# Gate products of a decoder step: one dense pair, seven pairs as seven-product units, projections ahead of them

## The chip, the cores and the metric

The kernel runs on one core of one Trainium2 chip. Its engines are TensorE (PE: matmuls and transposes into PSUM), VectorE (DVE), ScalarE (ACT), GpSimd (POOL) and SyncE (SP); SP and POOL also issue the DMA transfers. Each engine works through its own list of instructions in order and waits on semaphores. The metric is the device time of one execution in microseconds; the number of a kernel is the median of several executions.

## The reference

One inference step of a decoder layer on 1024 prompt positions and 8 sample tokens (1032 columns), model width 1024, all in fp32:

```python
xn = rmsnorm(x)
z = xn @ w_in                          # q, k, v | u, v_a | g_a | g_b
a_out = u * (tril(W_s) v_a + b)        # in chunks of 128 positions, 512 wide
b_out = dilated window attention       # 256 wide; sample tokens read caches
merged = sigmoid(ga) * (a_out @ w_proj_a) + sigmoid(gb) * (b_out @ w_proj_b)
h = x + merged @ w_out
up = rmsnorm(h) @ w_up                 # then a causal convolution of width 3
h = h + (gelu(gate) * val) @ w_down
y = rmsnorm(h)
```

The change is in the line `merged`: ga and gb are 1024 x 1032 each, made from 8 blocks of 128 output rows.

## The kernel before

Activations lie transposed: 128 features on the partitions, 1032 positions on the free axis; width 1024 is 8 such rows (KT = 8). An fp32 product is made of three matmuls (high x high, high x low, low x high), so each weight tile `wraw` is split by ACT into `whi` (a cast, L187) and by DVE into `wlo` (a subtraction, L188), and each operand likewise (`xnh`/`xnl`, `ah`/`al` for branch A, `bh`/`bl` for branch B, `mh` for the merged rows). `unit` (L208 to 210) runs one block of columns over all k; `dense` runs the blocks of a whole row: 384, 384 and 264 columns (`TB`), or 512, 260 and 260 (`TP`).

The up projection uses another form, `pair_unit` (L275 to 278). Two blocks of output rows are made together as a 2 x 2 block product in seven products in place of eight, in the order of `ORDER`: the weights enter as four parts and four sums (`ws`, L251; s1 to s4), the operand as blocks 11, 12, 21, 22 and the differences t1 to t4 (`tx`, L325), all split into `xc` tiles (cast L333 on ACT, subtraction L334 on DVE) by `combos`, after `scale_rows` (L307) has multiplied the rows by the norm. Columns come in two halves p (`HALF`) of 2 x 256 and 2 x 260 columns. Each of the seven products is 2 halves x 4 k x 3 matmuls of 256 or 260 columns; one unit is 168 matmuls.

The gate stage runs per block j: `gate` for g_a, then the projection of `a_out` with w_proj_a (4 k) whose eviction multiplies by the gate; after all eight, branch B's rows are split (`bh`, `bl`; the 8 sample columns come from `osam` by a transpose `bst`, copied to `bs`), and the eight g_b gates follow with w_proj_b (2 k) between them. Their evictions multiply, add and split the merged rows into `mh`. Then the output product, `h_pass(0)` and `h_pass(1)`.

Other work is cut into steps in the queue `side`; `tick` takes steps from it at the rate `pace` while the products are written out, and `drain` takes all that are left. In the gate stage these steps are the attention of the sample tokens: `load_keys` (tiles `ck`, `cq` from the caches), `key_scores` (L833, L834), `sample_softmax` (`sp`, L841 to L845), `sample_turn` (`pp`, `pT`), `load_values`, `sample_product` (`pv`, an ACT copy `os` and four small POOL stores to `osam`) and `sample_out` (`bst`). A scheduler then sets the order on each engine from the program's order and its data. `touch` (L92) is a copy of one element on DVE: it makes a DMA into a reused tile wait for the tile's last reader. PSUM is two rings of four banks, `pmm` for products and `pxx` for the rest; wraw has 3 buffers, whi and wlo 6 each.

## Time and profile before

| | us |
|---|---|
| median of 3 executions | 1525.52 (1525.44 to 1526.32) |
| profiled execution, whole | 1525.51 |
| its span, first to last instruction | 1523.8 |
| PE busy | 1500.1 (98%) |
| DVE busy | 901.1 (59%) |
| ACT busy | 590.2 (39%) |
| POOL busy | 114.3 (7%) |

In the chain of work that ended last PE holds 94%, DMA 3%, DVE 2%. The start-to-start distance of matmuls is the cost of a matmul; the duration in a row is longer, since matmuls overlap.

### The profile page before, as it was taken

Reading aid. Unit: us, or ns where it says so; the run is one execution under the profiler, and the core shown is the slowest. Engines: PE = TensorE matmul, PEld = TensorE weight load, DVE = VectorE, ACT = ScalarE, POOL = GpSimd, SP = SyncE. Lnnn points to the kernel's source line nnn. Section 1 sums busy time; section 2 is a strip of 40 time slices with the busy share of each in tenths; the row PEclk is TensorE's granted clock in tenths of the full one; section 3 lists DMA queues with packets and bytes.
Section 4 is the critical chain, followed back from the end, with each engine's and each line's share of the span. In section 5 each row is a group of like instructions: output and inputs, shape, how many; then the busy total and the mean of one; then the engine's idle time right before and its main releaser. Section 6 shows DMA issues by size and latency. Waiting matters only on the chain.

```text
span 1523.8 us, 25982 instructions
## 1 busy us (share of the span) xinstructions
PE 1500.1 (98%) x10518; PEld 1435.9 (94%) x10518; DVE 901.1 (59%) x1768; ACT 590.2 (39%) x1223; POOL 114.3 (7%) x275
## 2 busy tenths in 40 slices
PE   7999999999999999999999999999999999999997
PEld 7988999899999799998899999999999999899997
DVE  5444435435757224545687887878788856534436
ACT  6444333344121212333456655444445542212114
POOL 1100123132000200002000300000000001000000
PEclk9999999999999999999999999999999999999999
DMA  8300122133116311126443322222222246423302
GB/s 253 117 19 29 54 73 79 46 83 107 36 39 187 101 40 49 39 59 204 143 140 105 91 67 74 84 83 72 83 84 84 77 127 216 119 75 90 117 22 112
DMA packets 169420, 140.11 MB, mean 92 GB/s; under 512 B 7394, under 2 KB 154053, under 8 KB 169293
## 3 DMA queue, kind: packets, MB, share of 16 engines
q1 hardware_dynamic: 160277, 115.41, 25.0%
q0 software_dynamic: 8992, 23.04, 5.0%
q8 instruction: 82, 1.34, 0.4%
q14 instruction: 37, 0.30, 0.1%
q10 hardware_dynamic: 32, 0.01, 0.0%
HBM read 107.97 MB, written 30.68 MB: 91 GB/s over the span
## 4 chain that ended last, share of the span: by engine, by line
PE 94%; DMA 3%; DVE 2%; ACT 1%; issue 1%; SPq 0%; ACTq 0%; DVEq 0%
PE mm L208 19%; PE mm L209 19%; PE mm L210 19%; PE mm L277 8%; PE mm L275 8%; PE mm L278 8%; PE s L561 2%; PE po L586 2%; PE pt L576 1%; DMA gt<-g_d 1%; DMA x<-in_x_prompt_dram 1%; PE mm L711 1%; PE pv L871 1%; PE mm L713 1%; PE mm L712 1%; PE mm L1420 1%
## 5 line engine op out<-in xcount | busy, mean ns | idle before, releaser
L187 ACT CAST whi<-wraw 128x512 fp32r<-128x512 f32 (+2 forms) x275 | 158.4, 586 | 390.8 <-PE mm L209 281.1
L208 PE MATMUL mm<-xnh,whi 128*128 128x384 f32 (+3 forms) x936 | 308.6, 330 | 0.0
L277 PE MATMUL mm<-xc,whi 128*128 128x256 f32 (+1 forms) x1064 | 300.4, 282 | 0.0
L278 PE MATMUL mm<-xc,wlo 128*128 128x256 f32 (+1 forms) x1064 | 300.3, 282 | 0.0
L275 PE MATMUL mm<-xc,whi 128*128 128x256 f32 (+1 forms) x1064 | 300.2, 282 | 0.0
L210 PE MATMUL mm<-xnh,wlo 128*128 128x384 f32 (+3 forms) x936 | 299.6, 320 | 0.0
L209 PE MATMUL mm<-xnl,whi 128*128 128x384 f32 (+3 forms) x936 | 299.6, 320 | 0.0
L188 DVE TENSOR_TENSOR wlo<-wraw,whi 128x512 fp32r<-128x512 f32 (+2 forms) x275 | 174.2, 643 | 71.4 <-ACT whi L187 67.6
L277 PEld LDWEIGHTS mm<-xc,whi 128*128 128x128 f32 x1064 | 201.2, 189 | 0.0
L275 PEld LDWEIGHTS mm<-xc,whi 128*128 128x128 f32 x1064 | 201.1, 189 | 0.0
L278 PEld LDWEIGHTS mm<-xc,wlo 128*128 128x128 f32 x1064 | 200.8, 189 | 0.0
L208 PEld LDWEIGHTS mm<-xnh,whi 128*128 128x128 f32 x936 | 176.1, 188 | 12.3 <-issue 6.8
L209 PEld LDWEIGHTS mm<-xnl,whi 128*128 128x128 f32 x936 | 176.2, 188 | 3.7 <-issue 0.7
L210 PEld LDWEIGHTS mm<-xnh,wlo 128*128 128x128 f32 x936 | 175.9, 188 | 3.6 <-issue 0.7
L208 PE MATMUL mm<-gh,whi 128*128 128x384 f32 (+1 forms) x456 | 146.2, 322 | 4.7 <-ACT gh L1340 4.7
L209 PE MATMUL mm<-gl,whi 128*128 128x384 f32 (+1 forms) x456 | 147.3, 323 | 0.9 <-DVE gl L1341 0.8
L210 PE MATMUL mm<-gh,wlo 128*128 128x384 f32 (+1 forms) x456 | 146.4, 321 | 0.0
L1372 DVE TENSOR_TENSOR hD<-mm,hD 128x384 f32<-128x384 f32 (+1 forms) x96 | 48.0, 509 | 84.5 <-PE mm L210 84.3
L1312 DVE SCALAR_TENSOR_TENSOR cv<-up,cw,cv 128x1024 f32<-128x1024 f32 x76 | 97.1, 1278 | 0.8 <-issue 0.8
L208 PEld LDWEIGHTS mm<-gh,whi 128*128 128x128 f32 x456 | 86.4, 190 | 5.5 <-ACT gh L1340 5.5
L187 ACT CAST whi<-ws 128x512 fp32r<-128x512 f32 x76 | 47.2, 621 | 108.6 <-PE mm L277 107.4
L209 PEld LDWEIGHTS mm<-gl,whi 128*128 128x128 f32 x456 | 86.7, 190 | 1.7 <-DVE gl L1341 1.1
(295 smaller groups left out, 2599.0 us busy)
## 6 DMA issues: line engine op xcount, KB each, us to landing
wraw<-in_w_up_dram SPq DMA_DIRECT2D x50, 512.0 KB
wraw<-in_w_in_dram SPq DMA_DIRECT2D x42, 512.0 KB
gt<-g_d SPq DMA_DIRECT2D x22, 516.0 KB
g_d<-cv SPq DMA_DIRECT2D x19, 516.0 KB
wraw<-in_w_out_dram SPq DMA_DIRECT2D x16, 512.0 KB
wraw<-in_w_down_dram SPq DMA_DIRECT2D x24, 320.0 KB
xT_d<-xT POOLq DMA_DIRECT2D x8, 516.0 KB, 5.3
hD<-hT_d POOLq DMA_DIRECT2D x8, 516.0 KB, 7.4
```

Source lines behind the costliest of these rows:

```text
L187: nc.scalar.copy(hi[:, :n, :], src)
L188: nc.vector.tensor_tensor(lo[:, :n, :], src, hi[:, :n, :].bitcast(F32), op=ALU.subtract)
L208: nc.tensor.matmul(ps[:, :n], hi[k], xh, start=(k == 0), stop=False)
L209: nc.tensor.matmul(ps[:, :n], hi[k], xl, start=False, stop=False)
L210: nc.tensor.matmul(ps[:, :n], lo[k], xh, start=False, stop=(k == nk - 1))
L275: nc.tensor.matmul(ps, hi[:, k, :], xh, start=(first and k == 0), stop=False, skip_group_check=not first)
L277: nc.tensor.matmul(ps, hi[:, k, :], xl, start=False, stop=False, skip_group_check=not first)
L278: nc.tensor.matmul(ps, lo[:, k, :], xh, start=False, stop=(k == 3), skip_group_check=not first)
L561: nc.tensor.matmul(ps[:, off:off + ncol], qf[hr, qc:qc + P], kf[hr, kc:kc + ncol], start=True, stop=True)
L586: nc.tensor.matmul(po[:, gi * 64:gi * 64 + 64], pt[:, j * P:(j + 1) * P], vt[:, n, 64 * h:64 * h + 64], start=(bi == 0), stop=(bi == nb - 1))
L1312: nc.vector.scalar_tensor_tensor(c[:, :m], up[:, i:i + m], wi, c[:, :m], op0=ALU.mult, op1=ALU.add)
L1372: nc.vector.tensor_tensor(hT[j][:, cs], ps[:, :n], hT[j][:, cs], op=ALU.add)
```

## The change

The gates of block 0 stay as they were (both dense now with `TB`). For the blocks 1 to 7 the pair (g_a, g_b) of one block is one seven-product unit on the normalised x. Its operand `xn` is made in the same way as that of the up projection: rows of x are read back from memory (`xT_d` into `xr`, on SP), scaled by norm and `rb`, and turned into 28 `xc` tiles and the differences `tx`, as steps of `side` during the projections.

All eight products with w_proj_a, then all eight with w_proj_b, now come ahead of these units (`project`). The projected rows of blocks 1 to 7 are copied out of PSUM by ACT (`pr`) and stored to memory (`pa_d`, `pb_d`), and read back (`pl`) in the unit of their block, where two sigmoids, two multiplications and an addition over 1032 columns merge them. The merged rows are stored to `m_d`, read back by halves and split into `mh` while unit 7 and the first output pass run. The convolution parameters and histories move from the projections to the units; the rows of branch B become steps (`b_rows`). The function `pair_unit` is the same as for the up projection.

```diff
-            if (name, p, q) not in tsum:
+            if (id(X), name, p, q) not in tsum:
...
-    ma = []
-    ma.append(gate(3328))
-    for j in range(KT):
-        if j + 1 < KT:
-            ma.append(gate(3328 + (j + 1) * P))
-        if j == 0:
-            while len(a_hi) < 4:
-                side.popleft()()
-            pace[1] = 1.0
-            side.append(conv_params)
-            side.append(lambda: (load_hist(0), load_hist(1)))
-            side.append(lambda: None)
-            for i in range(6):
-                side.append(lambda i=i: turn_hist(i))
-            side.append(sample_out)
-        w = load_w(w_proj_a[0], 0, 4, j * P)
-        def post(b, t0, n, ps, sg=ma[j]):
-            nc.vector.tensor_tensor(sg[:, t0:t0 + n], ps[:, :n], sg[:, t0:t0 + n], op=ALU.mult)
-        dense(w, a_hi, a_lo, post)
...
+    sg0 = [gate(3328), gate(4352)]
+    while len(a_hi) < 4:
+        side.popleft()()
+    xR = [{}, {}]
+    xn = {}
+    def load_rows(R, p, i, src, after, ks=(0, 1)):
+        t0, n = HALF[p]
+        R[p][i] = ftile("xr")
+        touch(R[p][i], after)
+        for k in ks:
+            nc.sync.dma_start(R[p][i][:, 2 * k * n:(2 * k + 2) * n], src[2 * i + k][:, t0:t0 + 2 * n])
+    def x_loads(p, q):
+        for i in (q, q + 2):
+            load_rows(xR, p, i, xT_d, a_hi[3].bitcast(F32))
+    def x_steps(p, q):
+        yield lambda: x_loads(p, q)
+        yield idle
+        yield lambda: scale_rows(xR, p, q, (0, 1), lambda kt: nrm[:, kt:kt + 1], rb)
+        for names in (("11", "t1"), ("t2", "21"), ("t3", "22"), ("t4",)):
+            yield lambda names=names: combos(xn, xR, p, q, names)
...
-    mt = []
-    for j in range(KT):
-        sg = gate(4352 + j * P, False)
-        w = load_w(w_proj_b[0], 0, 2, j * P)
-        mj = [ftile("mh", F32R) for _ in range(2)]
-        def post(b, t0, n, ps, sg=sg, mj=mj, ma_j=ma[j]):
-            cs = slice(t0, t0 + n)
-            nc.vector.tensor_tensor(sg[:, cs], ps[:, :n], sg[:, cs], op=ALU.mult)
-            nc.vector.tensor_tensor(sg[:, cs], sg[:, cs], ma_j[:, cs], op=ALU.add)
-            mh, ml = m_parts(mj, t0, n)
-            nc.scalar.copy(mh, sg[:, cs])
-            nc.vector.tensor_tensor(ml, sg[:, cs], mh.bitcast(F32), op=ALU.subtract)
-        dense(w, b_hi, b_lo, post, blocks=TP)
-        mt.append(mj)
+    first_steps = list(side) + [sample_out, lambda: b_rows(0), lambda: b_rows(1)]
+    side.clear()
+    second_steps = [s for p in range(2) for q in range(2) for s in x_steps(p, q)]
+    late = max(0, len(first_steps) - 14)
+    side.extend(first_steps[:late])
+    for i in range(max(len(first_steps) - late, len(second_steps))):
+        side.extend(first_steps[late + i:late + i + 1])
+        side.extend(second_steps[i:i + 1])
+    pace_for(48)
+    m_d, pa_d, pb_d = (dpool.tile([KT, P, T], F32, tag=name, name=name) for name in ("m_d", "pa_d", "pb_d"))
+    def project(w2d, nk, ahi, alo, dst, first):
+        for j in range(KT):
+            w = load_w(w2d, 0, nk, j * P)
+            pr_ = first if j == 0 else ftile("pr")
+            def post(b, t0, n, ps, j=j, pr_=pr_):
+                cs = slice(t0, t0 + n)
+                if j == 0:
+                    nc.vector.tensor_tensor(pr_[:, cs], ps[:, :n], pr_[:, cs], op=ALU.mult)
+                else:
+                    nc.scalar.copy(pr_[:, cs], ps[:, :n])
+            dense(w, ahi, alo, post)
+            if j > 0:
+                nc.sync.dma_start(dst[j], pr_[:, :T])
+    project(w_proj_a[0], 4, a_hi, a_lo, pa_d, sg0[0])
+    while len(b_hi) < 2:
+        side.popleft()()
+    project(w_proj_b[0], 2, b_hi, b_lo, pb_d, sg0[1])
+    nc.vector.tensor_tensor(sg0[0][:, :T], sg0[0][:, :T], sg0[1][:, :T], op=ALU.add)
+    nc.sync.dma_start(m_d[0], sg0[0][:, :T])
+    drain()
+    side.append(conv_params)
+    side.append(lambda: (load_hist(0), load_hist(1)))
+    side.append(idle)
+    for i in range(6):
+        side.append(lambda i=i: turn_hist(i))
+    pace[1] = 1.0
+    mt = [[None, None] for _ in range(KT)]
+    mR = [{}, {}]
...
+    def m_steps(p, after):
+        side.append(lambda: [load_rows(mR, p, i, m_d, after, (0, 1) if i < 3 else (0,)) for i in range(4)])
+        side.append(idle)
+        for k in range(KT - 1):
+            side.append(lambda k=k: m_split(k, p, row_of(mR, p, k)))
+    def merge(sg, pl, cs):
+        for t in sg:
+            nc.scalar.activation(t[:, cs], t[:, cs], AF.Sigmoid)
+        for t, u in zip(sg, pl):
+            nc.vector.tensor_tensor(t[:, cs], t[:, cs], u[:, cs], op=ALU.mult)
+        nc.vector.tensor_tensor(sg[0][:, cs], sg[0][:, cs], sg[1][:, cs], op=ALU.add)
...
+    for j in range(1, KT):
+        wa, wb = (load_raw(win, 0, KT, c0 + j * P) for c0 in (3328, 4352))
+        sg = [ftile("sg") for _ in range(2)]
+        pl = []
+        def load_projected(j=j, sg=sg, pl=pl):
+            for src in (pa_d, pb_d):
+                t = ftile("pl")
+                touch(t, sg[0])
+                nc.gpsimd.dma_start(t[:, :T], src[j])
+                pl.append(t)
+        def outs(p, sg=sg):
+            t0, n = HALF[p]
+            return [t[:, t0:t0 + 2 * n] for t in sg]
+        side.appendleft(load_projected)
+        side.appendleft(idle)
+        side.appendleft(idle)
+        if j == KT - 1:
+            pace_for(7, 9)
+            m_steps(0, sg[0])
+        pair_unit(wa, wb, xn, outs)
+        if j < KT - 1:
+            while not pl:
+                side.popleft()()
+            merge(sg, pl, slice(0, T))
+            nc.sync.dma_start(m_d[j], sg[0][:, :T])
+        else:
+            drain()
+            for p in range(2):
+                t0, n = HALF[p]
+                cs = slice(t0, t0 + 2 * n)
+                merge(sg, pl, cs)
+                m_split(j, p, sg[0][:, cs])
...
+    m_steps(1, sg[0])
...
+    pace_for(8)
     h_pass(0)
+    drain()
+    pace[1] = 1.0
```

The order in which the instructions stand on the engines differs at three places. The first is PE at the end of the sample tokens' softmax. `sp` are the transposes of the scores, `pp` those of the probabilities, `mm` products with `xnh`/`xnl` gates and with `ah`/`al` a-projections. Before, around the first `pp` (the last score transpose stands further ahead):

```order
L208 MATMUL mm_862_5019<-xnh_14_118,whi_857_5010 128x384
L209 MATMUL mm_862_5019<-xnl_22_126,whi_857_5010 128x384
L210 MATMUL mm_862_5019<-xnh_14_118,wlo_858_5011 128x384
L851 MATMUL pp_845_4907<-ident_75,pr_3220 128x32
L208 MATMUL mm_862_5019<-xnh_15_119,whi_857_5010 128x384
L209 MATMUL mm_862_5019<-xnl_23_127,whi_857_5010 128x384
```

In the changed kernel, the same place:

```order
L840 MATMUL sp_839_4826<-ident_75,sc_3219 32x67
L208 MATMUL mm_862_4957<-ah_766_4367,whi_856_4931 128x384
L851 MATMUL pp_854_4917<-ident_75,pr_3220 128x32
L209 MATMUL mm_862_4957<-al_767_4368,whi_856_4931 128x384
L210 MATMUL mm_862_4957<-ah_766_4367,wlo_857_4932 128x384
```

One matmul is left between the last `sp` and the first `pp`. On ACT the exponential stands, in the changed kernel, ahead of the copies of the projections that end at that time (`pr_844` and later):

```order
L1168 COPY pr_836_4797<-mm_840_4835 128x264
L843 ACT_TABLE_LOAD
L843 ACTIVATE pr_3220,sm_3221<-sp_839_4826,sm_3221 32x323
L1168 COPY pr_844_4860<-mm_845_4861 128x384
L333 CAST xc_850_4895<-xr_827_4758 128x2x256
```

Before, no copy of a projection stood on ACT. The second place is PE where the sample columns of branch B are transposed (`bst`), before in the middle of a gate:

```order
L209 MATMUL mm_909_5411<-xnl_23_127,whi_904_5402 128x384
L210 MATMUL mm_909_5411<-xnh_15_119,wlo_905_5403 128x384
L883 MATMUL bst_910_5418<-ident_75,osam_3224 128x8
L883 MATMUL bst_911_5421<-ident_75,osam_3224 128x8
L208 MATMUL mm_909_5411<-xnh_16_120,whi_904_5402 128x384
```

and in the changed kernel behind the last sample product (`pv`) and ahead of the transposes `bps` and the first b-projection:

```order
L871 MATMUL pv_890_5145<-cv_848_4877,pT_3222 4x256
L883 MATMUL bst_895_5176<-ident_75,osam_3224 128x8
L883 MATMUL bst_896_5179<-ident_75,osam_3224 128x8
L1136 MATMUL bps_901_5191<-ident_75,oA_119_684 128x128 x4
L1136 MATMUL bps_902_5198<-ident_75,oA_119_684 128x128 x4
L1136 MATMUL bps_908_5217<-ident_75,oA_210_1183 128x128 x4
L1136 MATMUL bps_909_5224<-ident_75,oA_210_1183 128x128 x4
L208 MATMUL mm_913_5239<-bh_899_5189,whi_911_5235 128x384
L209 MATMUL mm_913_5239<-bl_900_5190,whi_911_5235 128x384
```

The gate matmuls around the transposes are gone. The third place is new: DVE behind the first b-projection, where the touches that release the loads of the second-half rows of x (`xr_916`, `xr_917`) stand behind the first eviction (L1166):

```order
L334 TENSOR_TENSOR xc_914_5244<-tx_903_5207,xc_914_5244 128x2x256
L1166 TENSOR_TENSOR sg_776_4434<-mm_913_5239,sg_776_4434 128x384
L92 COPY xr_916_5255<-ah_794_4566 1x1
L92 COPY xr_917_5259<-ah_794_4566 1x1
L1166 TENSOR_TENSOR sg_776_4434<-mm_915_5251,sg_776_4434 128x384
L1166 TENSOR_TENSOR sg_776_4434<-mm_918_5267,sg_776_4434 128x264
L307 SCALAR_TENSOR_TENSOR xr_916_5255<-xr_916_5255,nrm_115,rb_38_142 128x520
```

and ACT at the end of the b-projections, where the cast of the last weight sum of the first unit (`ws_1016`, the sum s4) stands ahead of the last copy of the last projection and of the first copy of the unit:

```order
L1168 COPY pr_984_5543<-mm_985_5544 128x384
L1168 COPY pr_984_5543<-mm_986_5552 128x384
L187 CAST whi_1017_5763<-ws_1016_5761 128x512
L1168 COPY pr_984_5543<-mm_987_5560 128x264
L280 COPY sg_990_5575<-mm_994_5581 128x256
```

## Rows read from the trace of the kernel before

**Rows 1.** Page, parts 1 and 2: busy time, granted clock by fortieths.

```profile
PE 1500.1 (98%) x10518; PEld 1435.9 (94%) x10518; DVE 901.1 (59%) x1768; ACT 590.2 (39%) x1223; POOL 114.3 (7%) x275
...
PEclk9999999999999999999999999999999999999999
```

**Rows 2.** Windows: us, busy (instructions) of each engine, PEclk, DMA share, GB/s.

```profile
455.00:590.00 135.00, 134.75 (x853) 124.22 (x852) 58.87 (x119) 29.74 (x49) 10.86 (x22) 1.00 0.36 99
590.00:703.00 113.00, 113.00 (x722) 102.71 (x721) 58.70 (x119) 34.61 (x73) 0.58 (x1) 1.00 0.19 55
865.00:1246.00 381.00, 381.00 (x3193) 381.00 (x3192) 305.83 (x495) 191.54 (x345) 9.16 (x76) 1.00 0.26 82
```

**Rows 3.** Timeline of PE, end of projection 0 and a gate: start, duration.

```profile
463.31 0.28 PE L210 MATMUL mm<-ah,wlo 128*128 128x264 f32 x1
...
465.52 0.34 PE L208 MATMUL mm<-xnh,whi 128*128 128x384 f32 x1
465.70 0.34 PE L209 MATMUL mm<-xnl,whi 128*128 128x384 f32 x1
...
470.61 0.28 PE L208 MATMUL mm<-xnh,whi 128*128 128x264 f32 x1
470.73 0.28 PE L209 MATMUL mm<-xnl,whi 128*128 128x264 f32 x1
```

**Rows 4.** Line L275: ns min/median/max, first and last start, forms.

```profile
L275 PE MATMUL mm<-xc,whi x1064: 277/282/289, 865.5 to 1246.3; 128*128 128x256 f32 x89, 128*128 128x260 f32 x89
```

**Rows 5.** Timeline of PE: last score transpose, first transpose of probabilities.

```profile
493.11 0.22 PE L840 MATMUL sp<-ident,sc 67*32 67x67 f32 x1
497.22 0.25 PE L851 MATMUL pp<-ident,pr 32*128 32x32 f32 x1
```

**Rows 6.** Timeline of ACT in that gap.

```profile
494.33 1.28 ACT L843 ACT_TABLE_LOAD   x1 [1.76 <-DVE sm L842]
495.63 0.52 ACT L843 ACTIVATE pr<-sp,sm 32x323 f32<-32x323 f32 x1
```

**Rows 7.** Timelines of DVE: runs of scalings, splits of rows, splits of weights.

```profile
755.67 2.08 DVE L307 SCALAR_TENSOR_TENSOR hT<-hT,nrm,acc 128x512 f32<-128x512 f32 x3 [0.95 <-ACT acc L1205]
764.32 1.89 DVE L334 TENSOR_TENSOR xc<-hT,xc 128x512 fp32r<-128x512 f32 x3
...
475.93 1.27 DVE L188 TENSOR_TENSOR wlo<-wraw,whi 128x512 fp32r<-128x512 f32 x2
```

**Rows 8.** Window of the key loads: us, PEclk, DMA share, GB/s; L834.

```profile
465.00:483.00 18.00, 1.00 1.03 274
...
L834 DVE TENSOR_REDUCE sc<-ck x6: 1196/1212/1221, 469.6 to 491.4; 128x16 f32<-128x1024 f32 x4, 67x16 f32<-67x1024 f32 x2
```

**Rows 9.** Timelines of ACT and POOL, tile osam: the last sample stores.

```profile
513.66 0.58 ACT L874 COPY os<-pv 4x512 f32<-4x512 f32 x1 [6.55 <-PE pv L871]
514.53 1.98 POOL L877 DMA_DIRECT2D osam<-os  x4 [1.15 <-ACT os L874]
DMA to landing us min/median/max: 1.5/1.6/3.9
L883 PE MATMUL bst<-ident,osam x2: 200/211/222, 548.5 to 548.6; 8*128 8x8 f32 x2
```

**Rows 10.** Timelines of PE and ACT: transposes and casts of branch B.

```profile
587.34 1.91 PE L1134 MATMUL bps<-ident,oA 128*128 128x128 f32 x16
587.97 2.06 ACT L1136 CAST bh<-bps 128x512 fp32r<-128x512 f32 x4
```

**Rows 11.** Tile hT: landing of the loads of x ahead of the output pass.

```profile
DMA to landing us min/median/max: 3.0/6.7/8.4
```

**Rows 12.** Timeline of PE and a window (PE busy, PEclk, DMA, GB/s), down stage.

```profile
1300.97 0.44 PE L208 MATMUL mm<-gh,whi 128*128 128x384 f32 x1 [2.69 <-ACT gh L1340]
...
1303.04 0.52 PE L208 MATMUL mm<-gh,whi 128*128 128x384 f32 x1
1303.36 0.52 PE L209 MATMUL mm<-gl,whi 128*128 128x384 f32 x1
...
1303.00:1304.00 1.00, 1.00 (x4) 0.50 0.09 14
```

More of the change, by code (lines that the diff above doesn't have):

```diff
@@ L318, in block @@
                 return t[:, :4 * n].rearrange("p (k b c) -> p b k c", k=2, b=2)[:, int(name[1]) - 1]
-            if (name, p, q) not in tsum:
+            if (id(X), name, p, q) not in tsum:
                 i = int(name[1]) - 1
                 if i % 2 == 0:
-                    tsum["tile", p, q] = ftile("tx")
-                t = tsum["tile", p, q][:, (i % 2) * 2 * n:(i % 2 + 1) * 2 * n].rearrange("p (k c) -> p k c", k=2)
+                    tsum[id(X), "tile", p, q] = ftile("tx")
+                t = tsum[id(X), "tile", p, q][:, (i % 2) * 2 * n:(i % 2 + 1) * 2 * n].rearrange("p (k c) -> p k c", k=2)
                 x, y = (("12", "11"), ("22", "t1"), ("22", "12"), ("21", "t2"))[i]
                 nc.vector.tensor_tensor(t, block(x), block(y), op=ALU.subtract)
-                tsum[name, p, q] = t
-            return tsum[name, p, q]
+                tsum[id(X), name, p, q] = t
+            return tsum[id(X), name, p, q]
         for name in names:
@@ L1072, in load_hist @@
         sf = ftile("sf")
-        touch(sf, a_hi[3].bitcast(F32))
+        touch(sf, osam)
         nc.gpsimd.dma_start(sf[:16, :nt * P], st2[:, c * P:(c + nt) * P])
@@ L1086, in turn_hist, with gate @@
         nc.scalar.copy(hist[:, c:c + nt, :], ps[:, :nt * 16].rearrange("p (f c) -> p f c", c=16))
-    def gate(c0, whole=True):
+    def gate(c0):
         w = load_w(win, 0, KT, c0)
@@ L1095, in post, with b_rows @@
             nc.vector.tensor_tensor(sg[:, cs], ps[:, :n], rb[:, cs], op=ALU.mult)
-            if b == 2 and whole:
+            if b == 2:
                 nc.scalar.activation(sg[:, :T], sg[:, :T], AF.Sigmoid)
-            elif not whole:
-                nc.scalar.activation(sg[:, cs], sg[:, cs], AF.Sigmoid)
-        dense(w, xn_hi, xn_lo, post, blocks=TB if whole else TP)
-        return sg
-    ma = []
-    ma.append(gate(3328))
-    for j in range(KT):
-        if j + 1 < KT:
-            ma.append(gate(3328 + (j + 1) * P))
-        if j == 0:
-            while len(a_hi) < 4:
-                side.popleft()()
-            pace[1] = 1.0
-            side.append(conv_params)
-            side.append(lambda: (load_hist(0), load_hist(1)))
-            side.append(lambda: None)
-            for i in range(6):
-                side.append(lambda i=i: turn_hist(i))
-            side.append(sample_out)
-        w = load_w(w_proj_a[0], 0, 4, j * P)
-        def post(b, t0, n, ps, sg=ma[j]):
-            nc.vector.tensor_tensor(sg[:, t0:t0 + n], ps[:, :n], sg[:, t0:t0 + n], op=ALU.mult)
-        dense(w, a_hi, a_lo, post)
-    drain()
+        dense(w, xn_hi, xn_lo, post)
+        return sg
+    sg0 = [gate(3328), gate(4352)]
[18 more added lines that the diff above has]
+            yield lambda names=names: combos(xn, xR, p, q, names)
     b_hi, b_lo = [], []
-    for hp in range(2):
+    def b_rows(hp):
         bh = ftile("bh", F32R)
@@ new lines, with m_split @@
+    mt = [[None, None] for _ in range(KT)]
+    mR = [{}, {}]
+    def m_split(k, p, src):
+        t0, n = HALF[p]
+        mt[k][p] = ftile("mh", F32R)
+        mh, ml = m_parts(mt[k], t0, 2 * n)
+        nc.scalar.copy(mh, src)
+        nc.vector.tensor_tensor(ml, src, mh.bitcast(F32), op=ALU.subtract)
+    def m_steps(p, after):
[3 more added lines that the diff above has]
+            side.append(lambda k=k: m_split(k, p, row_of(mR, p, k)))
@@ L1166 @@
             h = ftile("hT")
-            touch(h, mt[2 * i + 1][0].bitcast(F32))
+            touch(h, sg[0])
             hR[p].append(h)
@@ L1246, in h_mixed @@
                 side.append(lambda q=q, names=names: combos(hn, hR, p, q, names))
+    pace_for(8)
     h_pass(0)
+    drain()
+    pace[1] = 1.0
     h_steps(0)
```

1 line of the change is left out of this document (added).

## The prediction

> **What bounds the kernel now.** I read the page's busy shares first, then the windows by stage, then TensorE's timeline. PE is busy for 1500.1 us of 1523.8 and its granted clock is full in every slice [rows 1]. In the gate stage it is busier still: 134.75 of 135 us, then 113 of 113, and the up stage, which already runs the seven-product form, is full too [rows 2]. DVE is at 44%, 52% and 80% of those windows and ACT lower, so a change that takes matmul time away pays in full, but only as long as nothing makes PE wait; and the gate stage today keeps PE fed because there is always another gate whose operands are ready. The sum below is therefore: matmul time removed, minus stalls that appear when the ready gates are taken out from between the other work. The profiled run took 1525.51 us, 1.7 more than its span, and is at the median (1525.52), so I add to that.
>
> **Matmul time removed.** A 384-column matmul starts 0.175 us after the one before, a 264-column one 0.12 [rows 3]. A gate has 24 of each block: 24 x (0.175 + 0.175 + 0.1215) = 11.3 us, two gates 22.6. The seven-product unit: 19 units of the up stage, 1064 / 56, run from 865.5 to 1246.3 [rows 4], 20.04 us each. Seven pairs save 7 x (22.6 - 20.04) = **18.1 us**. The projections keep their counts (36 matmuls, 5.65 us, for an a block; 18, 2.83 us, for a b block), and the row count of PE in the changed program rises by what 7 x 168 against 14 x 72 asks. The pair units ask ACT and DVE for what the up units ask (a split of seven weight parts, four sums, the evictions), less the convolution; that stage is dense at 80% DVE, so I cost units 2 to 7 at nothing beside PE. Their rows (pa_d, pb_d, m_d, 516 KB each) are 1.6 MB a unit beside 1 MB of weights, 130 GB/s over 20 us, where the queues moved 274 [rows 8]. The history loads and transposes lie in the pair units now, hidden in the same way. The merged rows come back for half 0 under unit 7 and for half 1 under the first output pass: a landing of 3.0 to 8.4 us [rows 11] and seven splits of 0.6 on ACT and DVE fit in 20 us; if they didn't, that handover would cost about 5.
>
> **Stall 1, the softmax among the a-projections.** Today the third score transpose is at 493.11 and the first transpose of the probabilities at 497.22 [rows 5]: 4.1 us, spent on the maximum, a table load of 1.28, the exponential of 0.52 and its sum, and the normalisation [rows 6], while PE runs gate matmuls. In the new order exactly one 384-column matmul (0.175 us) stands between them, and every later copy of a projection on ACT stands behind the exponential. So PE waits for nearly the whole chain. Two things change its length. DVE now has scalings of the x rows ahead of and inside it: one scaling costs 0.69 in a run of them [rows 7], about 1 us in all, as two of the four fall under the table load and the exponential. And the scores must be there: the key and query loads keep the 16 DMA engines full from 465 to 483 [rows 8] and end about there, two DVE passes of 1.2 us follow, so 486; PE gets there at 486.1: the projection of block 0 ends at 463.4 [rows 3], four a blocks of 5.65 follow, and the 2.1 us of a 384-column block of the next one make up for the 2.1 that the order has put ahead of 463.4. Nothing is added for lateness. Bounds: 4.1 (scalings all covered) to 7 (the x rows land late, behind a 0.5 MB store, and hold the maximum up by 2 more). I take **5**, nearer the measured 4.1.
>
> **Stalls 2 and 3, from the last sample product to the first pair unit.** Today the last four sample stores are issued from 514.53 after an os copy at 513.66, and land 1.6 us after issue; the transposes that need them are only at 548.5 [rows 9], with gates in between. In the new order those transposes follow the last sample product directly, and all b-projections follow them. With 0 at the end of that product:
> - os copy 0.25 + 0.57, hand-over 0.3, the last issue 1.5 later, landing 1.6: 4.2. Transposes, bs copies, first bh casts (0.5 each [rows 10]): first b-projection matmul at 6.5.
> - Its second head pair stands on DVE behind nine instructions of about 0.6 (bl, and the subtractions of the first-half rows): 12. The eviction (0.55) and the touches behind it come at 13, and only these touches release the loads of the second-half x rows.
> - Four loads of 260 KB: the first lands after 3.0 [rows 11], at 16.
> - From there DVE is the bound. Up to the last weight sum of the first pair unit it has 8 scalings x 0.69 = 5.5, 22 subtractions and splits of 520 columns and 9 weight sums and splits of 512 at 0.63 (three in 1.89, two in 1.27 [rows 7]) = 19.5, two short splits 0.7, the merge of block 0 at 1.2: 26.9. In the middle it waits for the next two loads, which are again released by touches of its own: 3.0 and 0.5 for the issue, less 1.2 of sums: 2.3. Last sum at 45.2.
> - ACT's cast of this sum (0.62) stands ahead of the last copy of the last projection (0.4), and that copy frees the bank that the second half of product s1 needs. PE goes on at **46.2**.
> In this stretch PE has 16 transposes (1.75), eight b-blocks (22.6) and three half-products of 12 x 0.119: 28.6 us. So it loses **17.6 us**, some 6 before the b-projections and the rest in the first unit. Bounds: 12, if the loads land at once and DVE's chain is a tenth shorter; 24, if both groups of loads take the 6.7 that is the median of such loads in a queue [rows 11].
>
> **The clock.** After 2.69 us without work PE ran its next 384-column matmuls at intervals of 0.32 instead of 0.175, the granted clock being 0.50 (1.2 GHz) for about 3 us, and was back at full speed afterwards [rows 12]. Nine such intervals cost 1.3 us. I charge this after stall 1 and after the first unit's stall: 2.6. After stall 2 it falls under DVE's chain and costs nothing.
> The Trainium skill, "TensorE: Matmul & The Clock Gate", Part 1, has the same two levels and says that an idle array drops to the lower and has to work its way back. The row agrees. By the page every long gap pays, the one of stall 2 too, which I cost at nothing; with it the sum below would be 1.3 more, 1533.9.
>
> **Sum.** -18.1 + 5 + 17.6 + 2.6 = +7.1: **1532.6 us**. With all low bounds and no clock charge it is -18.1 + 4.1 + 12 = -2; with all high ones and five charged gaps (6.5) -18.1 + 7 + 24 + 6.5 = +19.4. The likeliest case alone spans 1526 to 1542.
>
> **Rivals.**
> *The saving shows.* Place: the first pair unit. The loads of the second-half rows wait, by the order, on touches behind the first b-eviction, but the rows they replace are long done and the DMA queues are idle then. If the chain before them is short (the b-rows ready at 4.2 and not behind the splits) and DVE's work spreads under the 22.6 us of b-projections, stall 3 falls from 11 to 1 or 2 and the sum is -18.1 + 5 + 6 + 2 + 1.3 = -4: 1521.7; with stall 1 covered as well 1516. It decides where stalls and clock together stay under 15 us. For it: DVE is at 44 to 52% in these windows. Against it: it needs 27 us of DVE in a row after a load that comes late.
> *No change that can be measured.* Stalls of 15 to 21 us, each term near its low bound: within 0.2% (3 us) of 1525.5, which is about what a measurement of this kernel tells from no change. For it: the low bounds are measured rows, and hand-summed chains tend to overcharge overlaps.
> *Clock and handover on top.* Stall 2 and stall 3 break into four or five gaps, each paid at the half clock because the DVE chain is not the only bound, and the merged rows are late for the first output pass (5): 1532.6 + 4 + 5 = 1541. For it: PE waits in that stretch for at least four different producers. Against: the output pass needs the last row some 5 us after it is there by my count.
> *The change doesn't do what it says*, and block products aren't taken for the gates: excluded by the order on PE.
>
> **How the numbers follow.** Forecast 0.45, clock and handover 0.15 (both slower), no change 0.18, saving shows 0.22. Of the forecast's case nearly all lies above 1528.6. Faster 0.22, same 0.18, slower 0.60. For 8 in 10 I leave out the far half of the first rival (below 1517) and the far part of the third (above 1541).
>
> **What would show it.** In the profile after: seven units of 20.0 us where the L277 group grows from 1064 to 1456; PE idle of about 5 us ahead of the first pp transpose, released by DVE L845 or ACT L843; about 6 us at bst and the first bh matmul, released by the sample stores, ACT bh and DVE bl; about 11 us in the first pair unit, released by ACT's copies and casts, with DVE back to back in it; a granted clock under 1 behind these gaps; no idle time at the start of the output pass. It is wrong if DVE finishes the second-half rows while the b-projections still run, if the sample chain overlaps the projections, or if PE idles in units 2 to 7.

## The result and the profile after

| | before, us | after, us |
|---|---|---|
| median of 4 executions | 1525.92 (1525.44 to 1526.74) | 1541.43 (1538.24 to 1544.14) |
| profiled execution, whole | 1525.51 | 1538.24 |
| its span | 1523.8 | 1536.4 |

The changed kernel is slower: the ratio is 1.0099 (95% interval 1.0082 to 1.0116), 15.5 us by the medians and 12.7 by the two profiled executions. The profiled one was the fastest of the four; the trace can explain 12.7 us, not the 3 us that lie between it and the median. The mean granted clock of each execution is on record: 0.989 in the profiled one, 0.987 in the other three. A difference of 0.002 of 1540 us is 3 us, so more time at the lower clock would fit the gap, but no trace of the other three shows it.

The page of the changed kernel, busy times and granted clock, beside [rows 1]:

```profile
PE 1490.9 (97%) x10686; PEld 1434.8 (93%) x10686; DVE 960.2 (62%) x1858; ACT 647.3 (42%) x1348; POOL 121.9 (8%) x289
...
PEclk9999999999999989999999999999999999999999
```

PE has 168 matmuls more, as predicted, and 9 us less of busy time. That isn't the whole saving, because matmuls at the lower clock last longer: one slice of the clock's row has dropped, the one around 560 us. The windows of the changed kernel from the end of the first a-projection to the end of the output product show where (columns as in [rows 2]):

```profile
463.40:488.00 24.60, 24.30 (x156) 23.82 (x154) 17.07 (x29) 5.47 (x12) 0.00 (x0) 1.00 1.02 287
488.00:500.00 12.00, 7.04 (x25) 5.51 (x26) 10.28 (x23) 6.02 (x12) 0.00 (x0) 0.72 1.02 327
500.00:523.00 23.00, 23.00 (x126) 15.50 (x124) 6.53 (x13) 7.79 (x18) 5.96 (x12) 1.00 0.44 138
523.00:537.00 14.00, 7.58 (x40) 7.00 (x39) 9.64 (x20) 6.94 (x15) 1.98 (x4) 0.76 0.37 116
537.00:562.00 25.00, 15.50 (x80) 14.64 (x79) 23.93 (x43) 13.41 (x28) 0.00 (x0) 0.84 0.56 191
562.00:580.00 18.00, 18.00 (x130) 18.00 (x130) 9.00 (x19) 10.76 (x24) 2.59 (x5) 0.94 0.61 207
580.00:720.00 140.00, 139.99 (x1160) 137.79 (x1159) 91.86 (x160) 65.07 (x127) 8.41 (x16) 1.00 0.46 143
720.00:863.00 143.00, 141.53 (x1019) 132.97 (x1018) 108.03 (x214) 76.80 (x143) 12.03 (x25) 1.00 0.54 169
```

PE idles 0.3 + 5.0 us around the softmax, 6.4 behind the last sample product, 9.5 in the b-projections and 1.5 in the output product, and the granted clock is under 1 in four of the windows, from 488 to 580 us with one full one between. The seven units (from 570.1 us to 715.6) are full. The view of PE's waits from 455 to 870 us names the releasers (total us, times, longest):

```profile
PE mm L208 <- ACT pr L1168: 13.2, 3, 5.3
PE bst L883 <- DMA osam<-os: 6.4, 2, 6.1
PE sp L840 <- DVE sc L834: 1.4, 1, 1.4
```

The kernel before has 0.2 us of such waits in its gate stage. On PE's timeline these are the short one at `sp` and the four long ones (start, duration; in brackets the idle time before and what ended it):

```profile
489.07 0.23 PE L840 MATMUL sp<-ident,sc 67*32 67x67 f32 x1 [1.37 <-DVE sc L834]
493.19 0.69 PE L208 MATMUL mm<-ah,whi 128*128 128x384 f32 x1 [3.88 <-ACT pr L1168]
...
529.42 0.24 PE L883 MATMUL bst<-ident,osam 8*128 8x8 f32 x1 [6.14 <-DMA osam<-os]
...
549.22 0.69 PE L208 MATMUL mm<-bh,whi 128*128 128x384 f32 x1 [5.30 <-ACT pr L1168]
549.71 0.52 PE L209 MATMUL mm<-bl,whi 128*128 128x384 f32 x1
550.03 0.52 PE L210 MATMUL mm<-bh,wlo 128*128 128x384 f32 x1
...
561.26 0.69 PE L208 MATMUL mm<-bh,whi 128*128 128x384 f32 x1 [4.03 <-ACT pr L1168]
```

After a long one, matmuls of 384 columns stand 0.32 us apart (549.71 to 550.03) where the kernel before has 0.175 [rows 3]. Windows of one microsecond show the granted clock (us, PE busy, PEclk, DMA share, GB/s):

```profile
497.00:498.00 1.00, 1.00 (x4) 0.50 1.16 316
...
530.00:531.00 1.00, 1.00 (x5) 0.50 0.00 0
...
562.00:563.00 1.00, 1.00 (x4) 0.50 0.35 132
```

It is 0.50 (1.2 GHz) for 5.9, 4.3, 4.4 and 2.8 us behind the four waits, read from the first matmul to where the distance is that of the full clock again. An estimate from these stretches: half of each is lost, 2.9 + 2.1 + 2.2 + 1.4 = 8.6 us.

ACT's timeline says what the copies `pr` (L1168), which free PE's banks, stood behind:

```profile
490.87 1.28 ACT L843 ACT_TABLE_LOAD   x1 [10.70 <-DVE sm L842]
492.17 0.52 ACT L843 ACTIVATE pr<-sp,sm 32x323 f32<-32x323 f32 x1
492.69 0.45 ACT L1168 COPY pr<-mm 128x384 f32<-128x384 f32 x1
...
547.64 0.62 ACT L333 CAST xc<-tx 128x520 fp32r<-128x520 f32 x1 [1.62 <-DVE tx L325]
548.17 0.62 ACT L333 CAST xc<-xr 128x520 fp32r<-128x520 f32 x1
548.70 0.47 ACT L1168 COPY pr<-mm 128x384 f32<-128x384 f32 x1
...
560.21 0.62 ACT L333 CAST xc<-xr 128x520 fp32r<-128x520 f32 x1
560.74 1.13 ACT L1168 COPY pr<-mm 128x384 f32<-128x384 f32 x3
```

At 493 it was the exponential, which waited for DVE's maximum. At 549 and 561 it was the casts of the second-half x rows; and the cast at 547.64 had itself waited for a difference (`tx`, L325) that DVE works off in one unbroken run:

```profile
545.71 0.68 DVE L334 TENSOR_TENSOR xc<-tx,xc 128x520 fp32r<-128x520 f32 x1
546.32 0.68 DVE L334 TENSOR_TENSOR xc<-xr,xc 128x520 fp32r<-128x520 f32 x1
546.93 0.68 DVE L325 TENSOR_TENSOR tx<-xr,xr 128x520 f32<-128x520 f32 x1
547.54 0.68 DVE L325 TENSOR_TENSOR tx<-xr,tx 128x520 f32<-128x520 f32 x1
```

**Balance.** Saved 18.1; idle 5.3 + 15.9; clock 8.6; that is +11.7 at the first output matmul, which is 13.7 later than before (715.59 against 701.87). About 1 of the 2 that are missing is there from the start of the program, where the first loads were waited for 9.7 us against 8.7; the other I did not place. The up stage ends 15.9 later (1262.2 against 1246.3): 1.5 of waits in and behind the output product (0.5 for the merged rows `mh`, 0.7 for a weight split, 0.2 in the norm) and 0.7 that I did not place. Its rest takes 273.9 us against 277.2, with the wait for the first down rows (`gh`) at 3.3 us against 4.7. The end is 12.6 later.

### The profile page after: what moved, and what is told of

Read it like the earlier page. It is cut to its first block, busy times and chain, and to the rows that moved or that the text cites. A ratio compares the mean times of both kernels' runs of the same rounds, so it can differ in the third digit from the quotient of the medians.

```text
span 1536.4 us, 26731 instructions
## 1 busy us (share of the span) xinstructions
PE 1490.9 (97%) x10686; PEld 1434.8 (93%) x10686; DVE 960.2 (62%) x1858; ACT 647.3 (42%) x1348; POOL 121.9 (8%) x289
## 4 chain that ended last, share of the span: by engine, by line
PE 92%; DMA 3%; DVE 2%; ACT 1%; issue 1%; SPq 0%; POOL 0%; ACTq 0%; DVEq 0%
PE mm L208 16%; PE mm L209 15%; PE mm L210 15%; PE mm L275 11%; PE mm L278 11%; PE mm L277 11%; PE s L561 2%; PE po L586 2%; PE pt L576 1%; PE mm L711 1%; PE mm L713 1%; PE mm L712 1%; DMA gt<-g_d 1%; PE pv L871 1%; PE xps L381 1%
## 5 line engine op out<-in xcount | busy, mean ns | idle before, releaser
L275 PE MATMUL mm<-xc,whi 128*128 128x256 f32 (+1 forms) x1456 | 412.2, 283 | 0.0
L278 PE MATMUL mm<-xc,wlo 128*128 128x256 f32 (+1 forms) x1456 | 411.0, 282 | 0.0
L277 PE MATMUL mm<-xc,whi 128*128 128x256 f32 (+1 forms) x1456 | 409.9, 282 | 0.0
L277 PEld LDWEIGHTS mm<-xc,whi 128*128 128x128 f32 x1456 | 275.2, 189 | 0.0
L275 PEld LDWEIGHTS mm<-xc,whi 128*128 128x128 f32 x1456 | 274.6, 189 | 0.4 <-DVE sg L288 0.2
L278 PEld LDWEIGHTS mm<-xc,wlo 128*128 128x128 f32 x1456 | 274.7, 189 | 0.0
L208 PE MATMUL mm<-xnh,whi 128*128 128x384 f32 (+1 forms) x600 | 200.5, 334 | 0.0
L210 PE MATMUL mm<-xnh,wlo 128*128 128x384 f32 (+1 forms) x600 | 192.3, 320 | 0.0
L209 PE MATMUL mm<-xnl,whi 128*128 128x384 f32 (+1 forms) x600 | 192.2, 320 | 0.0
L209 PEld LDWEIGHTS mm<-xnl,whi 128*128 128x128 f32 x600 | 113.0, 188 | 1.0 <-issue 0.7
L210 PEld LDWEIGHTS mm<-xnh,wlo 128*128 128x128 f32 x600 | 112.8, 188 | 0.8 <-issue 0.7
L188 DVE TENSOR_TENSOR wlo<-ws,whi 128x512 fp32r<-128x512 f32 x104 | 71.8, 691 | 31.7 <-ACT whi L187 26.9
```

Of the source, the lines that this page charges most:

```text
L188: nc.vector.tensor_tensor(lo[:, :n, :], src, hi[:, :n, :].bitcast(F32), op=ALU.subtract)
L208: nc.tensor.matmul(ps[:, :n], hi[k], xh, start=(k == 0), stop=False)
L209: nc.tensor.matmul(ps[:, :n], hi[k], xl, start=False, stop=False)
L210: nc.tensor.matmul(ps[:, :n], lo[k], xh, start=False, stop=(k == nk - 1))
L275: nc.tensor.matmul(ps, hi[:, k, :], xh, start=(first and k == 0), stop=False, skip_group_check=not first)
L277: nc.tensor.matmul(ps, hi[:, k, :], xl, start=False, stop=False, skip_group_check=not first)
```

## The experiments

All stand beside the kernel before, run on the same chip (medians 1525.27 to 1526.67). "Changed" is the changed kernel. The theory behind the first ones: the gates used to cover two chains, that of the sample tokens and that of the x rows, and what the sum missed is the half clock behind the waits. The rival: the stalls themselves are worth more or less than they look, for instance because the queue of the x rows' loads or the order of the projections holds PE.

**e1_warm.** Throwaway matmuls of few rows in the first two waits, to keep the clock up:

```diff
+        dm = xtile("dm")
+        for i in range(19):
+            nc.tensor.matmul(dm[:4, :256], sc[:67, 2, 28:32], rb[:67, :256], start=True, stop=True)
...
+            for i in range(20):
+                nc.tensor.matmul(dm[:4, :256], os_[:4, 0:4], rb[:4, :256], start=True, stop=True)
```

> The changed kernel with 19 throwaway matmuls (4x256, result unused) between the last score transpose and the first transpose of the probabilities, which start when the last score is there, and 20 between the last copy os and the sample transposes bst. They lengthen no chain of data and only keep TensorE busy while it would wait. Theory (the stalls are paid twice, once as idle time and once as matmuls at 1.2 GHz afterwards, about 2.5 us after the softmax and 2 after bst): 2.5 to 4.5 us faster than the changed kernel, 1537 to 1539. Rival (the clock's share is small or hidden, idle time alone explains the loss): no change, 1541, or 1 to 2 slower.

1552.42 us, ratio 1.0183 (1.0159 to 1.0206): a miss. The fp32 matmuls stand in the trace as two each, so they outlast the waits and delay PE themselves, the second batch to 541.3 (line and tile of the batch; ns min/median/max, first and last start):

```profile
L881 PE MATMUL dm<-rb,os x40: 374/629/629, 528.5 to 541.3; 4*4 4x256 f32 x40
```

and a window in it:

```profile
534.00:536.00 2.00, 2.00 (x6) 0.63 (x5) 0.00 (x0) 0.00 (x0) 0.00 (x0) 0.50 0.00 0
```

This window matters more: PE is busy all the time, and the clock is at 0.50 nevertheless (it was 1.00 from 528 to 530, as the batch began). These matmuls of 4 rows by 4 columns did not hold it. The run decides nothing on the theory.

**e8_warm2.** The same with matmuls of the full array, sized to the waits:

```diff
+        for i in range(22):
+            nc.tensor.matmul(dm[:, :384], a_hi[0][:, :P], a_hi[0][:, :384], start=True, stop=True)
...
+            for i in range(45):
+                nc.tensor.matmul(dm[:, :256], xh[:, :P], xh, start=True, stop=True)
```

> The changed kernel with throwaway matmuls of full width in two waits: 22 of 384 columns (3.9 us) behind the last score transpose, where TensorE waited 4.1, and 45 of 256 columns (5.4 us) behind the last sample product, where it waited 6.4. The first attempt used small fp32 matmuls, each of which took two passes, so they outlasted the waits. Theory (each wait is paid a second time at the half clock, some 2.8 and 2.1 us): 1536 to 1539. Rival (the half clock behind the waits is hidden or belongs to other things): 1541 or slower.

1537.48 us, ratio 1.0071 (1.0055 to 1.0088): 3.9 less than changed by the medians. The windows show the clock up across both filled waits, and low only behind the two in the b-projections, which were left alone:

```profile
480.00:500.00 20.00, 18.45 (x110) 16.73 (x109) 17.36 (x30) 7.79 (x16) 0.00 (x0) 1.00 1.08 318
...
520.00:540.00 20.00, 17.99 (x120) 15.87 (x119) 15.59 (x32) 9.17 (x21) 1.98 (x4) 1.00 0.42 130
540.00:560.00 20.00, 10.58 (x50) 9.94 (x49) 19.21 (x33) 11.68 (x24) 0.00 (x0) 0.76 0.57 202
```

The medians alone are weak evidence: the intervals of the two ratios just overlap (changed begins at 1.0082), and the two profiled executions differ by only 0.4 us (1537.81 against 1538.24). The traces say more (the first b-projection in changed and in e8, then e8's last wait):

```profile
533.41 0.42 PE L208 MATMUL mm<-bh,whi 128*128 128x384 f32 x1
...
529.66 0.42 PE L208 MATMUL mm<-bh,whi 128*128 128x384 f32 x1
...
558.56 0.69 PE L208 MATMUL mm<-bh,whi 128*128 128x384 f32 x1 [4.12 <-ACT pr L1180]
```

By the first b-projection e8 is 3.75 us ahead. Up to there PE's idle time in changed (11.7 us from `sp` on) is about as long as e8's idle time and filling together, so this is the clock, of which 2.9 + 2.1 = 5.0 had been estimated. Behind it part is lost again: there is a new wait of 0.8 for `bh`, and the half clock behind the wait that ends at 558.56 lasts 5.6 us, where changed has 2.8 behind nearly the same wait (4.03). So the clock is a cost of its own, beside the wait; how much of it reaches the end seems to differ from one execution to the next. The four executions of e8 all have a mean clock of 0.993 and lie within 1.9 us, those of changed within 5.9.

**e2_nosample** and **e7_ctrl.** The sample attention's steps are not built in either (its rows of `osam` are zeros); e2 does this in the changed kernel, e7 in the kernel before.

```diff
-    side.append(lambda: load_keys(*gh[0]))
...
-    side.append(sample_softmax)
...
+    nc.vector.memset(osam, 0.0)
```

> The changed kernel without the sample tokens' cache attention: no key, query and value loads, scores, softmax and products; osam is set to zero, so branch B of the sample columns is zero. This also takes away about 11 us of matmuls of the product pv. Theory (the softmax and the sample stores are two of the three stalls): beside these 11 us, stall 1 (5.3 idle, 2.8 at half clock) and most of the wait at bst (6.4 and 2) go: 1541 - 11 - 8 - 6 = 1516, 1511 to 1521. Rival (the building of the x rows is the one bound of the whole stretch, and the rest only hides in front of it): only the matmuls or less are gained, 1530 or above.

> The kernel before without the sample tokens' cache attention (same parts left out as in the changed kernel without it, which took 1502.5). It tells what the change is worth where the sample chain is absent. Theory (block products save 18, the x rows cost one stall of about 5 idle and 2 to 3 at half clock): the control loses only its 11 us of small matmuls, 1514 to 1516, so that the change is worth -11 to -14 there. Rival (the sample chain costs the kernel before as much as the changed one, the comparison with 1541 was unfair): control at 1490 to 1500.

e2: 1502.47, ratio 0.9848 (0.9833 to 0.9863). e7: 1509.89, ratio 0.9889 (0.9873 to 0.9905). Both were faster than expected: the steps cost the kernel before 16.4 us and not only the 11 us of the products `pv`. The pair is what counts. Without the samples the change gains 7.4 us, with them it loses 15.5, so their chain is worth 23 us in the new order. One long wait is left in e2, that of the x rows (PE's waits, 455 to 870 us):

```profile
PE mm L208 <- ACT pr L1153: 5.1, 1, 5.1
```

The 23 us are more than the chain's own two waits with their clock (5.3 + 6.4 + 5.0 = 16.7): the waits in the b-projections shrink too, from 9.3 to 5.1, presumably because DVE and ACT come to the x rows earlier with the steps gone.

**e4_order.** The new order without the product form: projections first, and behind them the gates as dense gates; no x rows are made.

```diff
-    second_steps = [s for p in range(2) for q in range(2) for s in x_steps(p, q)]
+    second_steps = []
...
-        pair_unit(wa, wb, xn, outs)
+        sg = [gate(3328 + j * P), gate(4352 + j * P)]
```

> The new order alone: projections first, their rows and the merged rows through memory, but the seven pairs of gates as dense products as before; no x rows are read back or split and there are no block products. Theory (order costs stalls 1 and 2, the x rows cost stall 3, the block products save 18): against before stall 1 (5.3 + 2.8) and the wait at bst (6.4 + 2), nothing saved, no stall in the b-projections: 1526 + 16 = 1542, 1538 to 1546. Rival (the x rows alone cost what the block products save and more, the order is free): 1526 to 1530.

1536.63 us, ratio 1.0078 (1.0061 to 1.0094). The order alone costs 11 us, before any product form. That lies between the two forecasts: the softmax is waited for, but the wait at `bst` that the theory charged does not appear, and another one in the a-projections does. Its waits:

```profile
PE pp L851 <- DVE pr L845: 3.4, 1, 3.4
PE mm L208 <- ACT pr L1168: 3.0, 1, 3.0
```

From here to changed the product form takes off 18.1 and the sum still rises by 4.8, so by subtraction the x rows, made during the projections, cost 23 us with all that they delay, the wait at `bst` included.

**e6_pool.** The 14 subtractions of the second-half x rows on POOL, to relieve DVE:

```diff
-            nc.vector.tensor_tensor(v[:, 1], s, v[:, 0].bitcast(F32), op=ALU.subtract)
+            sub = nc.gpsimd if X is xn and p == 1 else nc.vector
+            sub.tensor_tensor(v[:, 1], s, v[:, 0].bitcast(F32), op=ALU.subtract)
```

> The changed kernel with the 14 low-part subtractions of the second-half x rows on POOL in place of DVE. Theory (stall 3, 9.5 us idle in the b-projections and 3.5 at half clock, is set by the chain of instructions on DVE from the landing of the second-half rows on, with ACT's casts and copies queued behind it): DVE's chain is 8.5 us shorter, the stall falls by 4 to 9: 1532 to 1537, less if POOL takes over 1.5 us for one. Rival (stall 3 is set by the landing of the loads or by ACT itself): no change, 1540 to 1543.

1545.91 us, ratio 1.0129 (1.0114 to 1.0144), a miss in sign. The row of POOL's subtractions of differences, then PE's waits:

```profile
L336 POOL TENSOR_TENSOR xc<-tx,xc x8: 1284/1644/1765, 550.3 to 570.7; 128x520 fp32r<-128x520 f32 x8
```

```profile
PE mm L208 <- ACT pr L1169: 15.6, 4, 7.3
PE bst L885 <- DMA osam<-os: 8.0, 2, 7.8
```

One takes 1.64 us there against 0.68 on DVE, and the waits behind ACT grow from 13.2 to 15.6. (Of the other six, subtractions of the rows themselves, the median is 1.75.) A slower maker of the x rows makes the stall longer; this supports, in the wrong direction for the kernel, that the chain of the x rows holds PE.

**e11_nop1.** The second-half x rows are not made; the units of the second half read the first half's tiles instead.

```diff
-    second_steps = [s for p in range(2) for q in range(2) for s in x_steps(p, q)]
+    second_steps = [s for q in range(2) for s in x_steps(0, q)]
```

> The changed kernel without building the second-half x rows: not loaded, scaled, differenced or split; the units read the first half's tiles in their place (same shapes and counts of matmuls; the gates of the second half of the columns are those of other data). Theory (the waits in the b-projections, 9.5 us idle and about 3.5 at half clock, are this building alone): 1541.4 - 13 = 1528, 1525 to 1531. Rival (the waits come from the copies of the projections, the weight sums or the transfers): 1536 or more.

1524.58 us, ratio 0.9991 (0.9982 to 1.0001): 16.8 less than changed, a little more than expected. The b-projections are now full, at the full clock; only the two waits of the sample chain are left (a window, then PE's waits):

```profile
537.00:562.00 25.00, 25.00 (x182) 25.00 (x182) 10.34 (x20) 14.49 (x32) 2.59 (x5) 1.00 0.76 261
```

```profile
PE pp L855 <- DVE pr L849: 4.9, 1, 4.9
PE bst L887 <- DMA osam<-os: 3.8, 1, 3.8
```

The 9.5 us of waits in the b-projections and their clock (3.6) thus come from the making of these rows; 2.6 more of the 16.8 is the wait at `bst`, shorter here (3.8 against 6.4), presumably since fewer steps stand in the queue. The run takes out the loads, DVE's work and ACT's casts together, so it doesn't say which of them holds PE. For DVE speaks that it is busy for 23.93 of 25 us in that window of the changed kernel, and ACT for 13.41. Even with half of the x rows for nothing the change only breaks even: of the 18.1, 8.7 us go to the two waits of the sample chain, and the clock behind them and what was not placed take the rest.

**e10_first** and **e9_first_split.** The order of the steps. e10 puts all sample steps ahead of the x rows; e9 does this too and takes the sample columns out of the b rows, so that the b-projections of the prompt columns start without `bst` and the last column block follows one block later.

```diff
-    late = max(0, len(first_steps) - 14)
+    late = len(first_steps) - 2
...
-            dense(w, ahi, alo, post)
+            dense(w, ahi, alo, post, tbs=(0, 1) if lag else (0, 1, 2))
```

> The changed kernel with another order of the queue: all steps of the sample attention first, then the steps of the x rows, instead of alternating. On TensorE the sample products then stand some 9 us earlier and the transposes bst inside the a-projections. Theory (the stall at bst is order alone): it goes with its half clock, 8.4 us, stall 1 stays, the rows come later and the last stall grows by up to 5: 1533 to 1539. Rival (DVE and ACT are the bound of the stretch as a whole, so what is won at bst is lost at the rows): 1540 to 1543.

> The order of the run before, and branch B's prompt rows are transposed and split ahead of the sample columns, which are only needed by the third block of a b-projection; that block is put one projection later, so bst stands behind the first b blocks. Theory: the last sample transposes get 4 us more cover; with stall 1 partly covered too (one more a block between scores and probabilities) 1530 to 1537, about 2 below the run with the order alone. Rival (the rows are the bound): equal to that run.

e10: 1539.51, ratio 1.0078 (1.0056 to 1.0099). e9: 1534.73, ratio 1.006 (1.004 to 1.008). In e10 the wait at `bst` falls from 6.4 to 0.4 us, and others appear; PE's waits:

```profile
PE mm L275 <- ACT xc L333: 6.3, 2, 4.1
PE mm L208 <- ACT pr L1168: 4.7, 2, 2.4
PE pp L851 <- DVE pr L845: 3.4, 1, 3.4
```

e10 lies between its two forecasts, e9 in its theory's range. Part of what the sample chain gives back, the x rows take, now inside the first pair unit too. Order moves the waits between the two chains.

**e13_act, e12_act_split, e14_act_bsplit.** Less work for DVE in the chain: the scaling by the norm is one ACT instruction per row, and `rb` is multiplied to the results of the units. e12 adds the whole of e9, e14 only its split of the b columns.

```diff
-        yield lambda: scale_rows(xR, p, q, (0, 1), lambda kt: nrm[:, kt:kt + 1], rb)
+                nc.scalar.activation(r, r, AF.Copy, scale=nrm[:, kt:kt + 1])
...
+            nc.vector.tensor_tensor(t[:, cs], t[:, cs], rb[:, cs], op=ALU.mult)
```

> The changed kernel with the x rows scaled by the norm's gain alone, on ACT, and the factor rb multiplied to the gates behind the units (two more DVE multiplications of 1032 columns a unit). In the critical stretch DVE loses 8 instructions of 0.69, ACT gains 8 of about 0.55. Theory (DVE's chain is the bound of the last stall, at 96% busy there, ACT at 54%): the stall shrinks by 3 to 5.5: 1535 to 1539. Rival (ACT's queue is the bound): 1541 to 1546.

> The same scaling on ACT in the version with the sample steps first and the b blocks split (1534.7). Theory: another 3 to 5.5 less, 1529 to 1532; it would have to lose 9 to reach the kernel before. Rival: no gain, 1534 to 1538.

> The scaling on ACT (1532.5) together with branch B's prompt rows ahead of its sample columns and the third b block one projection later, but the queue's order as in the changed kernel. Theory (the stalls add up, so a fix of one is worth its own size beside the other): the wait at bst of 3.8 us and its half clock shrink by 2 to 4, 1528 to 1531, still 2 to 5 above the kernel before. Rival (what is won at bst is given back at the rows, as in the run with the sample steps first): 1532 to 1535.

| | us | ratio |
|---|---|---|
| e13 | 1532.47 | 1.0043 (1.003 to 1.0056) |
| e12 | 1533.95 | 1.005 (1.0033 to 1.0066) |
| e14 | 1536.45 | 1.0072 (1.0055 to 1.0089) |

e13 is the fastest of the versions that compute the whole step, and still slower than the kernel before. Its waits:

```profile
PE mm L208 <- ACT pr L1172: 7.7, 2, 4.7
PE bst L883 <- DMA osam<-os: 3.8, 2, 3.7
...
PE pp L851 <- DVE pr L845: 1.0, 1, 1.0
```

The gain is larger than forecast, but not where the theory put it: the waits in the b-projections fall only from 9.3 to 7.7, by 1.6 and not by 3 to 5.5. The softmax's waits fall from 5.3 to 1.3 (1.0 at `pp`, 0.3 at `sp`) and that at `bst` from 6.4 to 3.8, as they would with the scalings of the x rows out of DVE's line. e12 is within 1 us of e9, so its forecast of 3 to 5.5 failed. In e14 `bst` is not waited for, but the other waits take its place (3.9 at the first `pp`, 9.2 in five waits behind `pr`, 3.3 for `bh`): the forecast of 1528 to 1531 took the waits as independent of one another, and they aren't.

Not tried: dense gates kept as cover between the projections. They would need the split rows `xnh` and `xnl` beside the 28 `xc` tiles; whether SBUF holds both, no run shows.

## Why the prediction was right in sign and too small

- **Matmul time removed, 18.1.** Right: 168 matmuls more, and the seven units full, in 145.5 us with the history transposes among them (7 x 20.04 = 140.3 alone), with DVE at 66% as hidden work. e4 and e11 bear the size out.
- **Stall 1, 5.** The size came out (5.3), in part by luck. 1.4 of it are lateness of the scores, for which the prediction added nothing: DVE's last product with the keys waited for its load until 486.55, where the prediction had the loads end at 483. From the last score transpose to the first `pp` it took 4.7 us (489.07 to 493.81) against 4.1 before, about what was charged, but PE idled for only 3.9 of it: the one matmul between them could run as soon as ACT's copy behind the exponential had freed its bank.
- **Stalls 2 and 3, 17.6.** The size was near (15.9 idle), by errors that offset. The first b-projection matmul came 10.3 us behind the last sample product and not 6.5: the last four os stores landed 4.1 to 4.8 us after issue instead of 1.6 [rows 9], and the 16 transposes took 3.5 us at the half clock instead of 1.9. The loads of the second-half rows, on the other hand, charged with 3.0 and 2.3, left no gap in DVE's run. That only the touches release them was wrong: three of the eight were issued ahead of their touches, two at 524.06 and one at 546.24, where the touches stand at 537.84 and 550.58. By the kernel, a touch writes one element at the start of a tile, and the load of the tile's second row doesn't cover it. The place was wrong: the third stall stood in the b-projections and not in the first pair unit. ACT's copies free the banks of every projection, so the queue behind the casts stops PE at whichever copy comes next; the prediction saw this at the last copy alone. One of its own signs of being wrong is there: DVE ends the splits of the second-half rows at 564.9, while the b-projections run until 570.1.
- **The clock, 2.6: the step that failed.** "After stall 2 it falls under DVE's chain and costs nothing", two charges of 1.3. All four waits were followed by matmuls at 1.2 GHz, for 2.8 to 5.9 us and not the 3 of [rows 12], 8.6 us in all; filling two of them gave 3.9 us back by the medians (e8). The path was wrong: the prediction let PE wait once, at the end of DVE's chain, so that slow matmuls ahead of that wait would cost nothing. The last weight sum of the first unit came when forecast, 45.6 us behind the last sample product against 45.2:

```profile
568.73 0.69 DVE L251 TENSOR_TENSOR ws<-wraw,ws 128x512 f32<-128x512 f32 x1
```

But PE did not wait for it. It had waited among the b-projections instead, each time with slow matmuls behind, and reached the unit only at 570.12. With the clock kept up behind stall 2, in e8, the waits in the b-projections were as long as in the changed kernel (9.4 us in two, against 9.3) and stood 2.4 to 2.7 us earlier, so the chain moved with PE. By the order it starts behind PE's transposes and first b-projection, and these were among the slow ones. The row that the price came from also held more than it said: between its wait of 2.69 us and the slow matmuls lie one matmul of 0.44 us (the first slow one behind a wait takes 0.69) and a second wait, of 0.82 us. The Trainium skill, "TensorE: Matmul & The Clock Gate", Part 1, by which every long gap pays, was the better guide here; the traces agree with it at all four gaps.
- **The merged rows, nothing.** Nearly right: 0.5 of the 1.5 us of waits in the output stage are for `mh`. The rival "clock and handover on top" had put 5 on it and 1541 on the sum; its several gaps with a clock charge each came true, its handover did not, so that its number is the measured one is luck in part.

With 8.6 for the clock and the measured waits the prediction's sum is -18.1 + 5.3 + 15.9 + 8.6 + 1.5 = +13.2, against 12.7 profiled; the down stage's -3.3 and the 2.7 of the balance that the change's steps don't explain nearly cancel. From the forecast of +7.1 to +12.7 it is 5.6 us: the clock, the step that failed, was 6.0 too low, and the other errors nearly cancel. That the median lies 3 us above the profiled execution stays open; the lower mean clock of the other executions fits it, but is not shown to be its cause.

## What to carry to other kernels

Ready work between latency chains is worth its cover, not only its own time: here 18 us of matmuls saved cost 21 us of waits and 9 us of clock. Price a wait on PE as its length plus half of the stretch that it runs at 1.2 GHz behind it, at every such gap (here 3.9 to 6.1 us long), and allow for a stretch that differs between executions. Where one engine both prepares the next stage and frees the banks of the current one, look at each copy in its queue and not only at the last; and expect reordered waits to reappear at the next chain, as e10, e12 and e14 showed.

## What the runs showed of the hardware

- With fp32 matmuls of 4 rows and 4 columns PE was busy for 2.00 of 2.00 us and the granted clock was 0.50 all the same (e1); through the batches of the full array it was 1.00 (e8).
- An fp32 matmul of 256 columns stands as two in the trace (19 issued, 38 recorded).
- The half clock lasted 2.8 to 5.9 us behind waits of 3.9 to 6.1 us, and a longer wait did not mean a longer stretch: 5.9 behind 3.9, 4.3 behind 6.1. Behind the same wait it differed between two executions: 2.8 us behind 4.03 (changed), 5.6 behind 4.12 (e8).
- POOL's subtraction of 128x520 took 1.64 us (median of e6's eight differences), 2.4 times the 0.68 on DVE.
